# The first dense block in two halves, and the S5 parameters loaded beside the modulation

## The chip, the cores and the metric

The kernel runs on one core of one Trainium2 chip. The metric is the device time of one execution in microseconds (us). Three runs of the kernel before took 3180.70, 3186.01 and 3205.12 us; the median is 3186.01 us.

## What is computed

One step of a decoder layer is computed for a prompt of 2048 tokens and for 8 x 8 sample tokens, width 1024, all in float32. Cut to what matters here:

```python
mod = silu(c) @ w_ada + b_ada                     # c: 9 rows (prompt and 8 samples), w_ada 1024 x 6144
sh1, sc1, gt1, sh2, sc2, gt2 = split(mod, 6)      # six pieces of 1024 columns
h = rms_norm(x, norm1_g) * (1 + sc1) + sh1
q, k, v, g, u, gate_r, gate_s = split(h @ w_in)
ret = retention(rotary(q), rotary(k), v)          # gated by silu(g)
ssm = s5(u, lam, log_dt, b, c, d)                 # diagonal state space scan, complex
x = x + gt1 * (merge of ret and ssm) @ w_out
x = x + gt2 * relu(rms_norm(x) * (1 + sc2) + sh2 @ w_up)**2 @ w_down
```

No `h` exists before `sh1` and `sc1` (columns 0 to 2047 of `mod`) are known, and the S5 branch needs tables (powers of exp(lam dt), and products with b and c) that are worked out from small parameters.

## The kernel before

The prompt is worked off in four super-blocks of 512 tokens; the feed-forward part comes behind all four. A product of float32 numbers is made of three products of rounded pieces: every operand X is kept as `hi`, X rounded to the matmul's type, and `lo`, the rest.

**Weights.** `fetch` loads one unit of a weight (256 x 512, 512 KB) into a tile `wraw`, of which there are four (RAW). `refill` makes `whi` from it on ScalarE (ACT, L191) and `wlo` by a subtraction on GpSimd (POOL, L194), or on VectorE (DVE, L194) for units of `w_ada`. `block` takes the units of one 512-column product, one after the other, for four PSUM banks `pd`: with eight input tiles of 128 rows there are four units of 24 matmuls, 96 in all. `self.names` is the order of the blocks: "u", "ada4", "q", "ada5", "k", "ada6", "v", "ada7", "g", and so on. All DMAs are issued by SyncE (SP), in order, and each waits for the one eight places before it (eight semaphores, DMAHW0 to DMAHW7, taken in turn).

**The start** is `setup`. It loads the columns of `w_ada` in four pieces of 512 (`load(n)`, two tiles `wa` of 1 MB each), and the first 512 rows of x (tiles `x0`, four loads of 512 KB, L1412). Pieces 0 and 1 give `sh1`, pieces 2 and 3 give `sc1`. The loop `for q in range(2)` does the two halves of the 1024 channels: `ada(q)` and `ada(2 + q)` are the modulation products on TensorE (PE, L810, into `ps_ada`), `mod_out` adds the bias on DVE (`mt`, L843), turns the result with PE (`ptm`, L848) and copies it to `modT` (L849); `scales` works out `s1`. For each of the four tiles of x, `turn` transposes four pieces into a bank `pt` (L817) and `norm_out` scales them on DVE (`m`, L651), rounds them on ACT (`hh`, L653) and subtracts on POOL (`hl`, L654). `hh[0], hl[0]` are the first half of the channels, `hh[1], hl[1]` the second. Rows of x are first brought to unit size by sums of squares on ACT (`junk`, L605), a short chain of one-column instructions on DVE (L591 to L610) and a multiplication (L825). Then `super_block` begins with block "u", all 96 matmuls over both halves.

**The S5 set-up** is a generator, `s5_setup`: small loads first (`lam`, `s5w` for log_dt, `s5bc`, `s5cc`, L906 to L921), then two PE steps (`pl` L927, `pc` L934), then about 300 instructions on DVE. The first of these, L943, needs log_dt alone; the chain to L1020 works on 32 or 64 columns; from L1034 on tables are built and eight steps (L1104 to L1132) make the tiles that go to DRAM. `setup` runs it to its first `yield`, behind everything else. The rest is spread over the blocks by the `spawn`ed filler.

**What sets the order.** The Python code gives the order in which instructions are written, but a scheduler reorders each engine's list by its own timeline before the program is built. Each engine then runs its list strictly in order, and a waiting instruction holds up all behind it. PSUM has two pools of four banks, `pd` for the dense products and `pm` for all else.

Of the kernel before, what the change touches and what calls it, by code (L numbers as in the profile page):

```python
# [10 lines left out]
F32 = mybir.dt.float32  # L11
# [6 lines left out]
P = 128  # L18
# [64 lines left out]
class Layer:  # L83
# [150 lines left out]

    def block(self, name, kind, src, evac=None, sample=None, order="k"):
        nc = self.nc
        assert self.names[self.at] == name, (self.names[self.at], name)
        self.at += 1
        nu = 2 if name == "glu" or name[:2] in ("br", "bs") else 4
        nk = 2 * nu  # L240
        banks = [self.pd.tile([P, 512], F32, tag="pd", name=f"pd_{name}") for _ in range(4)] if kind else []
        sb = self.bank(f"ps_{name}", [P, 512]) if sample else None
# [19 lines left out]
        if order == "k":  # L262
            for u in range(nu):
                w = self.weight(name)
                for j in range(4 if kind else 0):
                    for kk in range(2):
                        products(2 * u + kk, j, w, kk)
                    if u == nu - 1:
                        evac(j, banks[j])
                    if j == 0:  # L270
                        self.refills()
                    self.tick()
                if sample:
                    for kk in range(2):
                        sample_products(2 * u + kk, w, kk)
                    if u == nu - 1:
                        self.spawn(sample[1](sb))
                    if kind is None:
                        self.refills()
                        self.tick()  # L280
                self.due += 1
                self.side()
            return
# [449 lines left out]
    def setup(self):  # L733
# [30 lines left out]
        dma(gn[8:16], i["norm2_g"].rearrange("o (k p) -> (o k) p", p=P))  # L764
        wa = [self.unit("wa") for _ in range(8)]
        wv = i["w_ada"][0].rearrange("(k p) n -> p k n", p=P)

        def load(n):
            for a in range(2):
                dma(wa[2 * n + a], wv[:, 4 * a:4 * a + 4, 512 * n:512 * n + 512])  # L770

# [7 lines left out]
        for j in range(2, 4):  # L779
            self.x_rows(xu[1][:, j - 2], 0, j)  # L780
        load(1)
        load(3)
        for _ in range(RAW):
            self.fetch()

        th = self.work("th", [9, D])
# [20 lines left out]
        def ada(n):  # L807
            pa = self.pd.tile([P, 512], F32, tag="pd", name=f"ps_ada{n}")
            for k in range(8):
# [10 lines left out]
        for q in range(2):  # L820
            ada(q)
            if q == 0:
                for j in range(4):
                    r = self.now(self.row_rstd(x[j]))
                    V.tensor_scalar(x[j], x[j], r, None, op0=ALU.mult)  # L825
                pts = [turn(q, j) for j in range(4)]
            else:
                for _ in range(2):
                    self.refill(True)
            ada(2 + q)  # L830
            self.scales(2 + q)
            for j in range(4):
                pt = turn(q, j) if q else pts[j]
                self.norm_out(pt, q, self.s1[:, :, 0], self.modT[:, 0:8, 0], self.hh, self.hl, j, nc.gpsimd)
        for _ in range(RING - 2):
            self.refill(True)
        self.late_setup = self.s5_setup()
        next(self.late_setup)

    def mod_out(self, n, p, bias):  # L840
# [3 lines left out]
        if n in (4, 5, 10, 11):  # L844
            nc.sync.dma_start(self.modd[:, 512 * n:512 * n + 512], t)
        pt = self.pd.tile([P, 4, 9], F32, tag="pd", name="ptm")
        for a in range(4):
# [617 lines left out]
    def super_block(self, b, late):  # L1465
# [39 lines left out]
        if b == 0:  # L1505
            s5 = self.spawn(self.late_setup, 2)
        self.block("u", "T", srcT(hh, hl), ev_u, S(hS, ev_us))
        if b:
# [283 lines left out]
```

## Time and profile before

| | |
|---|---|
| median of three runs | 3186.01 us |
| the profiled execution's own time | 3184.32 us |
| its span, first to last instruction | 3182.5 us |
| PE busy | 2927.9 us (92%) |
| DVE, ACT, POOL busy | 1940.6 (61%), 1219.5 (38%), 1762.7 us (55%) |
| granted TensorE clock, mean | 0.955 |

A row of a timeline has the start in us, the duration, the engine, the line of the kernel, the operation, the tile written `<-` the tiles read, the shapes and a count; in brackets how long the engine was idle before it and what ended that. A row with a count spans all its instructions. SPq rows are the issues of DMAs; their durations are those of the issue, not of the transfer. The table by windows has for each stretch the busy time of each engine with its number of instructions, the granted clock of PE, and the busy share of the DMA engines.

### The profile page before, as it was taken

How to read it: one execution, taken by the hardware profiler on the slowest of the kernel's cores; microseconds unless marked ns; L12 is line 12 of the kernel's file. 1: busy time of each engine (PE TensorE's matmuls, PEld its weight loads, DVE VectorE, ACT ScalarE, POOL GpSimd, SP SyncE). 2: the span in 40 equal slices, each digit the busy share in tenths (PEclk: the TensorE clock that was granted, in tenths of full speed). 3: DMA queues.
4: the chain of work that ended last, by engine and by line, in shares of the span. 5: the costliest groups of instructions: out<-in, count | busy, mean ns of one | idle time of the engine just before them, and what ended most of it. 6: DMA issues, size and time to landing. Idle time of an engine off the chain costs nothing. (4 is left out here: it accounts for less than half of the span.)

```text
span 3182.5 us, 37110 instructions
## 1 busy us (share of the span) xinstructions
PE 2927.9 (92%) x13436; PEld 2384.8 (75%) x13436; DVE 1940.6 (61%) x3116; ACT 1219.5 (38%) x1876; POOL 1762.7 (55%) x1028
## 2 busy tenths in 40 slices
PE   7789999999989899999999669999999999997995
PEld 3568777788777688787788558887778788875884
DVE  4978674761667865657644745545556655456654
ACT  2233442122423234432244235555334555553332
POOL 2331454434345545555356456658888666587881
PEclk9889999999999899999999889999999999998998
DMA  8466435543246854367543654446444644466442
GB/s 218 154 196 208 147 103 171 162 130 109 85 107 212 240 174 136 105 200 229 162 137 127 183 163 168 155 146 205 159 146 167 203 166 158 159 219 210 143 148 82
DMA packets 335980, 516.51 MB, mean 162 GB/s; under 512 B 71206, under 2 KB 167990, under 8 KB 331691
## 3 DMA queue, kind: packets, MB, share of 16 engines
q1 hardware_dynamic: 335796, 514.13, 51.0%
q8 instruction: 106, 1.74, 0.2%
q14 instruction: 78, 0.64, 0.1%
HBM read 399.29 MB, written 114.78 MB: 162 GB/s over the span
## 5 line engine op out<-in xcount | busy, mean ns | idle before, releaser
L194 POOL TENSOR_TENSOR wlo<-wraw,whi 128x1024 fp32r<-128x1024 f32 x248 | 614.2, 2487 | 764.3 <-ACT whi L191 646.7
L399 PE MATMUL pq_down<-shi,tw 128*128 128x512 f32 x1792 | 568.9, 397 | 36.6 <-DVE acc L459 26.4
L399 PE MATMUL pq_up<-shi,tw 128*128 128x512 f32 x1792 | 558.5, 392 | 34.9 <-ACT shi L390 26.1
L191 ACT ACTIVATE whi<-wraw 128x1024 fp32r<-128x1024 f32 x312 | 324.0, 1056 | 651.0 <-issue 72.2
L399 PEld LDWEIGHTS pq_down<-shi,tw 128*128 128x128 f32 x1792 | 342.2, 191 | 115.9 <-issue 21.9
L399 PEld LDWEIGHTS pq_up<-shi,tw 128*128 128x128 f32 x1792 | 338.6, 189 | 108.3 <-ACT shi L390 28.4
L311 POOL TENSOR_TENSOR tw<-traw,tw 128x512 fp32r<-128x512 f32 x192 | 286.5, 1507 | 210.4 <-ACT tw L310 210.1
L391 DVE TENSOR_TENSOR slo<-sw,shi 128x1024 fp32r<-128x1024 f32 x140 | 236.9, 1704 | 209.6 <-ACT shi L390 177.4
L399 PE MATMUL pq_down<-slo,tw 128*128 128x512 f32 x896 | 354.1, 395 | 0.0
L399 PE MATMUL pq_up<-slo,tw 128*128 128x512 f32 x896 | 351.0, 392 | 1.7 <-DVE slo L391 1.7
L390 ACT ACTIVATE shi<-sw 128x1024 fp32r<-128x1024 f32 x140 | 147.1, 1056 | 271.2 <-DMA sw<-sd 181.2
L459 DVE SCALAR_TENSOR_TENSOR acc<-pq_down,modT,acc 128x512 f32<-128x512 f32 x224 | 159.2, 743 | 89.7 <-PE pq_down L399 89.3
L399 PEld LDWEIGHTS pq_up<-slo,tw 128*128 128x128 f32 x896 | 169.3, 189 | 38.0 <-DVE slo L391 3.0
L399 PEld LDWEIGHTS pq_down<-slo,tw 128*128 128x128 f32 x896 | 171.4, 191 | 35.2
L310 ACT ACTIVATE tw<-traw 128x512 fp32r<-128x512 f32 x224 | 136.3, 624 | 66.5 <-PE pq_down L399 51.5
L409 ACT ACTIVATE aq<-pq_up 128x512 f32<-128x512 f32 x128 | 72.3, 591 | 194.2 <-PE pq_up L399 194.2
L345 POOL TENSOR_TENSOR ts<-traw,ts 128x512 f32<-128x512 f32 x64 | 97.6, 1525 | 57.1 <-issue 54.6
L194 DVE TENSOR_TENSOR wlo<-wraw,whi 128x1024 fp32r<-128x1024 f32 x64 | 85.8, 1340 | 69.5 <-ACT whi L191 65.5
L311 POOL TENSOR_TENSOR tw<-t,tw 128x512 fp32r<-128x512 f32 x64 | 103.3, 1624 | 32.7 <-ACT tw L310 28.7
L310 ACT ACTIVATE tw<-ts 128x512 fp32r<-128x512 f32 x128 | 80.2, 627 | 101.1 <-PE pq_up L399 80.4
L253 PE MATMUL pd_wo<-whi,mh 128*128 128x512 f32 x256 | 102.2, 403 | 12.1 <-DVE tw L1680 6.7
L437 DVE TENSOR_TENSOR sq<-aq 128x512 f32<-128x512 f32 x32 | 29.6, 925 | 130.7 <-ACT aq L414 130.7
(526 smaller groups left out, 6770.9 us busy)
## 6 DMA issues: line engine op xcount, KB each, us to landing
wraw<-in_w_in_dram SPq DMA_DIRECT2D x144, 512.0 KB
sw<-sd SPq DMA_DIRECT2D x112, 512.0 KB
s5p<-s5c SPq DMA_DIRECT2D x32, 1024.0 KB
traw<-in_w_up_dram SPq DMA_DIRECT2D x64, 512.0 KB
sd<-sq SPq DMA_DIRECT2D x32, 1024.0 KB
sd<-aq SPq DMA_DIRECT2D x32, 768.0 KB
traw<-in_w_down_dram SPq DMA_DIRECT2D x24, 1024.0 KB
wraw<-in_w_ada_dram SPq DMA_DIRECT2D x32, 512.0 KB
```

The costliest lines, as they stand in the source:

```text
L191: a = nc.scalar.activation(hi, raw, AF.Copy)
L194: l = eng.tensor_sub(lo, raw, hi)
L253: nc.tensor.matmul(banks[j], a, b, start=(k == 0 and z == 0), stop=(k == nk - 1 and z == 2))
L310: self.nc.scalar.activation(t[:, 0], x, AF.Copy)
L311: eng.tensor_sub(t[:, 1], x, t[:, 0])
L345: G.tensor_sub(x[p], l, x[m] if isinstance(m, int) else m)
L390: nc.scalar.activation(hi[:, a], t, AF.Copy)
L391: V.tensor_sub(lo[:, a], t, hi[:, a])
L399: self.nc.tensor.matmul(bank, w, x, start=(first and a == 0 and z == 0), stop=(a == 3 and z == 2), skip_group_check=True)
L409: copy = lambda d, b: nc.scalar.activation(d, b, AF.Copy)
L437: V.tensor_add(S[:, 0], A21, A22)
L459: V.scalar_tensor_tensor(d, b, g, d, op0=ALU.mult, op1=ALU.add)
```

## The change

The first block is cut in two, and what surrounds it is put in another order.

- `block` gets an argument `part`. With `part=0` it takes the first two units of the weights (channels 0 to 511, `hh[0]` and `hl[0]`) and keeps its four banks; with `part=1` it takes the other two units into the same banks and finishes.
- In `setup`, `block("u", part=0)` is written behind the first half of the normalisation, ahead of `ada(1)` and `ada(3)`; `super_block` then does `part=1`.
- The loads of pieces 1 and 3 of `w_ada` move behind the S5 parameters; two units of u's weights are fetched ahead of both.
- `s5_setup` is begun in the middle of `setup`, and run on to its third `yield` within it.
- The products `ada(1)` and `ada(3)` and their `ptm` use the pool `pm` in place of `pd`, whose four banks the first half of u keeps.

```diff
+        if part != 0:
+            self.at += 1
...
+        if part == 1:
+            banks = self.held
+        else:
+            banks = [self.pd.tile([P, 512], F32, tag="pd", name=f"pd_{name}") for _ in range(4)] if kind else []
+            self.held = banks
...
-            for u in range(nu):
+            for u in range(nu) if part is None else range(2 * part, 2 * part + 2):
...
         for j in range(2, 4):
             self.x_rows(xu[1][:, j - 2], 0, j)
-        load(1)
-        load(3)
-        for _ in range(RAW):
+        for _ in range(2):
             self.fetch()
+        self.late_setup = self.s5_setup()
+        next(self.late_setup)
...
-            pa = self.pd.tile([P, 512], F32, tag="pd", name=f"ps_ada{n}")
+            pa = self.pm.tile([P, 512], F32, tag="pm", name=f"ps_ada{n}") if n % 2 else \
+                self.pd.tile([P, 512], F32, tag="pd", name=f"ps_ada{n}")
...
             ada(q)
             if q == 0:
+                load(1)
+                load(3)
+                for _ in range(RAW - 2):
+                    self.fetch()
                 for j in range(4):
                     r = self.now(self.row_rstd(x[j]))
                     V.tensor_scalar(x[j], x[j], r, None, op0=ALU.mult)
                 pts = [turn(q, j) for j in range(4)]
             else:
-                for _ in range(2):
-                    self.refill(True)
+                next(self.late_setup)
             ada(2 + q)
...
+            if q == 0:
+                next(self.late_setup)
+                for _ in range(2):
+                    self.refill(True)
+                hh, hl = self.hh, self.hl
+                self.block("u", "T", lambda k, j: (hh[k // 4][:, k % 4], hl[k // 4][:, k % 4]), part=0)
         for _ in range(RING - 2):
             self.refill(True)
-        self.late_setup = self.s5_setup()
-        next(self.late_setup)
...
-            s5 = self.spawn(self.late_setup, 2)
-        self.block("u", "T", srcT(hh, hl), ev_u, S(hS, ev_us))
+            s5 = self.spawn(self.late_setup, 1)
+        self.block("u", "T", srcT(hh, hl), ev_u, S(hS, ev_us), part=None if b else 1)
```

What the scheduler makes of it is seen in the lists of the engines. The changed kernel has other line numbers: from `s5_setup` on they are 15 higher (L943 is now L958), L843 and L849 are now L857 and L864, L810 and L817 are now L817 and L824, and L253 is now L258.

DVE before, from the last preparation of silu(c) on: the bias of the first modulation piece (`mt`) comes next.

```order
L800 TENSOR_TENSOR cT<-z,cT 128x8x9 [waits Activation_49]
L843 TENSOR_TENSOR mt<-ps_ada_176,ba 9x512 [waits DMAHW0_49,PE_49]
L849 COPY modT<-ptm 128x36 [waits PE_49]
L609 TENSOR_SCALAR v<-ss 128x1 [waits Activation_49]
L610 TENSOR_SCALAR v<-v 128x1 [waits DVE_49]
L591 TENSOR_SCALAR y<-v 128x1 [waits DVE_49]
```

DVE after, at the same place (`s5w` holds log_dt, and DMAHW4 is the landing of its load):

```order
L806 TENSOR_TENSOR cT<-z,cT 128x8x9 [waits Activation_49]
L958 TENSOR_SCALAR s5w<-s5w 128x32 [waits DMAHW4_49]
L857 TENSOR_TENSOR mt<-ps_ada_187,ba 9x512 [waits DMAHW0_49,PE_49]
L959 TENSOR_SCALAR s5w<-s5w 128x32 [waits DVE_49]
L960 CAST s5w<-s5w 128x32 [waits DVE_49]
L961 CAST s5w<-s5w 128x32 [waits DVE_49]
L864 COPY modT<-ptm 128x36 [waits PE_49]
L614 TENSOR_SCALAR v<-ss 128x1 [waits Activation_49]
```

The first instruction of the S5 chain now stands ahead of `mt` of the first modulation product, and the rest of that chain is woven into the normalisation of x.

SP before, from the load of the third tile of x on (`x_126` are tiles 2 and 3):

```order
L1412 DMA x_126<-in_x_prompt_dram 128x1x1024 [waits DMAHW4_49]
L1412 DMA x_126<-in_x_prompt_dram 128x1x1024 [waits DMAHW5_49]
L770 DMA wa<-in_w_ada_dram 128x4x512 [waits DMAHW6_49]
L770 DMA wa<-in_w_ada_dram 128x4x512 [waits DMAHW7_49]
L770 DMA wa<-in_w_ada_dram 128x4x512 [waits DMAHW0_49]
L770 DMA wa<-in_w_ada_dram 128x4x512 [waits DMAHW1_49]
L181 DMA wraw<-in_w_in_dram 128x2x512 [waits DMAHW2_49]
```

SP after, at the same place:

```order
L1427 DMA x_118<-in_x_prompt_dram 128x1x1024 [waits DMAHW4_49]
L1427 DMA x_118<-in_x_prompt_dram 128x1x1024 [waits DMAHW5_49]
L181 DMA wraw<-in_w_in_dram 128x2x512 [waits DMAHW6_49]
L181 DMA wraw<-in_w_in_dram 128x2x512 [waits DMAHW7_49]
L921 DMA lam<-in_ssm_lambda_re_dram 32x64 [waits DMAHW0_49]
L922 DMA lam<-in_ssm_lambda_re_dram 32x64 [waits DMAHW1_49]
L921 DMA lam<-in_ssm_lambda_im_dram 32x64 [waits DMAHW2_49]
L922 DMA lam<-in_ssm_lambda_im_dram 32x64 [waits DMAHW3_49]
L924 DMA s5w<-in_ssm_log_dt_dram 128x32 [waits DMAHW4_49]
L928 DMA s5bc<-in_ssm_b_re_dram 64x32x16 [waits DMAHW5_49]
```

Nine more S5 loads follow, and then the four `wa` of pieces 1 and 3. The load of log_dt stands eight places behind that of the third tile of x, so it waits for that tile.

PE before, from the transposes of the first two tiles of x on; `ps_ada_332` is `ada(1)`:

```order
L848 MATMUL ptm<-cpk,mt 128x9 [waits DVE_49]
L848 MATMUL ptm<-cpk,mt 128x9 x3
L810 MATMUL ps_ada_332<-wa,z 9x512 [waits DMAHW6_49]
L810 MATMUL ps_ada_332<-wa,z 9x512 x3
L810 MATMUL ps_ada_332<-wa,z 9x512 [waits DMAHW7_49]
L810 MATMUL ps_ada_332<-wa,z 9x512 x3
L817 MATMUL pt<-cpk,x_126 128x128 [waits DVE_49]
```

PE after, with `ps_ada_444` for `ada(1)`, which now lies in the pool `pm`, and the first rows of block "u":

```order
L949 MATMUL pc<-cpk,s5cc 128x128 [waits DMAHW4_49,DMAHW3_49]
L949 MATMUL pc<-cpk,s5cc 128x128 x3
L817 MATMUL ps_ada_444<-wa,z 9x512 [waits DMAHW6_49,DVE_49]
L817 MATMUL ps_ada_444<-wa,z 9x512 x3
L817 MATMUL ps_ada_444<-wa,z 9x512 [waits DMAHW7_49]
L817 MATMUL ps_ada_444<-wa,z 9x512 x3
L258 MATMUL pd_u<-hh,whi 128x512 [waits Activation_49]
L258 MATMUL pd_u<-hl,whi 128x512 [waits Pool_49]
```

`ada(1)` now stands behind all four transposes of x and the S5 transposes (`pl`, `pc`) and also waits for DVE, which must empty the last of the four `pt` banks first. The 48 matmuls of u's first half follow it, then `ptm` of `ada(1)`, all of `ada(3)`, and the transposes of the second half of the channels; the other 48 matmuls of u come last.

More of the change, by code (lines that the diff above doesn't have):

```diff
@@ L233, in side, with block @@
             self.spawn(evac(st[0]))
-    def block(self, name, kind, src, evac=None, sample=None, order="k"):
+    def block(self, name, kind, src, evac=None, sample=None, order="k", part=None):
         nc = self.nc
         assert self.names[self.at] == name, (self.names[self.at], name)
-        self.at += 1
+        if part != 0:
+            self.at += 1
         nu = 2 if name == "glu" or name[:2] in ("br", "bs") else 4
         nk = 2 * nu
-        banks = [self.pd.tile([P, 512], F32, tag="pd", name=f"pd_{name}") for _ in range(4)] if kind else []
+        if part == 1:
[3 more added lines that the diff above has]
+            self.held = banks
         sb = self.bank(f"ps_{name}", [P, 512]) if sample else None
@@ L764, in setup @@
         dma(gn[8:16], i["norm2_g"].rearrange("o (k p) -> (o k) p", p=P))
-        wa = [self.unit("wa") for _ in range(8)]
+        wa = {}
         wv = i["w_ada"][0].rearrange("(k p) n -> p k n", p=P)
@@ L769, in load @@
             for a in range(2):
+                wa[2 * n + a] = self.unit("wa")
                 dma(wa[2 * n + a], wv[:, 4 * a:4 * a + 4, 512 * n:512 * n + 512])
@@ L845, in mod_out @@
             nc.sync.dma_start(self.modd[:, 512 * n:512 * n + 512], t)
-        pt = self.pd.tile([P, 4, 9], F32, tag="pd", name="ptm")
+        pool = ("pm", self.pm) if n % 2 else ("pd", self.pd)
+        pt = pool[1].tile([P, 4, 9], F32, tag=pool[0], name="ptm")
         for a in range(4):
```

## The prediction

> **What bounds the kernel now.** I read the windows first, cut at the marks of the first blocks, then the timelines of PE, DVE, ACT and SP there.
>
> ```profile
> 0.00:62.90 62.90, 41.81 (x121) 11.91 (x121) 22.27 (x76) 12.36 (x25) 9.88 (x10) 0.89 0.84 237
> 62.90:86.60 23.70, 23.70 (x109) 18.96 (x109) 22.92 (x77) 11.05 (x15) 9.84 (x6) 1.00 0.71 170
> 86.60:222.60 136.00, 105.46 (x466) 83.50 (x465) 129.19 (x258) 36.43 (x48) 47.31 (x21) 0.85 0.51 167
> 222.60:300.00 77.40, 75.09 (x416) 61.21 (x415) 62.35 (x148) 26.58 (x42) 17.67 (x7) 0.97 0.76 240
> 300.00:3182.00 2882.00, 2681.85 (x12331) 2209.18 (x12329) 1703.86 (x2561) 1133.09 (x1748) 1677.97 (x984) 0.96 0.50 158
> ```
>
> The columns are the stretch, its length, busy PE, PEld, DVE, ACT and POOL, the clock, DMA share and GB/s. From 222.6 us on PE is busy 97% of the next stretch, so it sets the pace there. Before that it lacks work: 21.1 us up to 62.9 (62.90 - 41.81) and 30.5 us between 86.6 and 222.6 (136.00 - 105.46), where DVE is busy for 129.2 of 136.0 us. The start waits for loads and normalisation, the stretch behind it for DVE, which works through the S5 set-up. The change touches only these 222.6 us, and the idle PE there, some 52 us or 1.6% of the span, is the most that it could give.
>
> ```profile
> 9.84 9.66 PE L810 MATMUL ps_ada<-wa,z 128*9 128x512 f32 x16 [1.25 <-DVE z L798]
> 20.26 0.41 PE L848 MATMUL ptm<-cpk,mt 9*128 9x9 f32 x4 [0.77 <-DVE mt L843]
> 41.06 9.40 PE L810 MATMUL ps_ada<-wa,z 128*9 128x512 f32 x16 [2.77 <-DMA wa<-in_w_ada_dram]
> 52.52 0.66 PE L817 MATMUL pt<-cpk,x 128*128 128x128 f32 x4 [0.15 <-DVE m L651]
> 54.78 7.04 PE L810 MATMUL ps_ada<-wa,z 128*9 128x512 f32 x16
> 62.92 0.50 PE L253 MATMUL pd_u<-hh,whi 128*128 128x512 f32 x1
> 86.59 0.39 PE L259 MATMUL ps_ada<-whi,cT 128*41 128x512 f32 x1
> 90.26 0.40 PE L253 MATMUL pd_q<-hh,whi 128*128 128x512 f32 x1
> 139.97 0.80 PE L253 MATMUL pd_k<-hh,whi 128*128 128x512 f32 x1 [10.23 <-DVE rt L1518]
> 210.69 0.45 PE L1116 MATMUL pw<-cpk,s5bx 128*128 128x128 f32 x1 [8.02 <-DVE s5bx L1109]
> ```
>
> Block "u" runs from 62.92 to 86.59 without a gap; its first half hides the second half of the normalisation. Between 86.59 and 90.26 stand sixteen matmuls, 0.229 us each.
>
> ```profile
> 19.53 0.68 DVE L843 TENSOR_TENSOR mt<-ps_ada,ba 9x512 f32<-9x512 f32 x1 [9.18 <-PE ps_ada L810]
> 24.80 0.75 DVE L825 TENSOR_SCALAR x<-x,y 128x1024 f32<-128x1024 f32 x1
> 61.85 0.68 DVE L843 TENSOR_TENSOR mt<-ps_ada,ba 9x512 f32<-9x512 f32 x1 [6.77 <-PE ps_ada L810]
> 63.79 5.20 DVE L651 TENSOR_SCALAR m<-pt,s,modT 128x128 f32<-128x128 f32 x16
> 68.91 0.87 DVE L943 TENSOR_SCALAR s5w<-s5w 128x32 f32<-128x32 f32 x1
> 79.40 1.22 DVE L194 TENSOR_TENSOR wlo<-wraw,whi 128x1024 fp32r<-128x1024 f32 x1
> 104.94 0.68 DVE L868 TENSOR_TENSOR mt<-mt,ps_ada 9x512 f32<-9x512 f32 x1
> 105.74 0.69 DVE L1034 TENSOR_TENSOR s5pw<-s5bc,s5w 128x512 f32<-128x512 f32 x1
> 222.58 0.16 DVE L1191 COPY s5t<-carry 128x4 f32<-128x4 f32 x1
> ```
>
> DVE begins the S5 chain at 68.91, reaches its tables at 105.74 and is through at 222.58; block "g" and with it the dense stretch follow. So two chains must be compared: when DVE gets to L1034 and from there to L1191, and whether PE has its work done by then.
>
> **The change part by part.**
>
> *The new wait.* L943 now stands ahead of the first `mt` on DVE and waits for log_dt. That load cannot be issued before the third tile of x has landed, eight places ahead of it.
>
> ```profile
> 33.82 0.63 ACT L605 ACTIVATE junk<-x 128x512 f32<-128x512 f32 x1 [9.39 <-DMA x<-in_x_prompt_dram]
> 38.67 0.63 ACT L605 ACTIVATE junk<-x 128x512 f32<-128x512 f32 x1 [3.51 <-DMA x<-in_x_prompt_dram]
> 62.70 0.42 SPq L909 DMA_DIRECT2D s5w<-in_ssm_log_dt_dram  x1
> 63.16 0.69 SPq L913 DMA_DIRECT2D s5bc<-in_ssm_b_re_dram  x1
> 72.14 0.45 SPq L1504 DMA_DIRECT2D rot<-in_rot_dram  x1
> ```
>
> The third tile is there at 33.82. In the trace of before log_dt is issued at 62.70 and used at 68.91, at most 6.2 us later. The fourth tile of x, there at 38.67, and two units of weights are in the queues ahead of log_dt. Bounds: 34 + 2, if it overtakes them, to 38.7 + 6.2 = 45. I take **39**, the fourth tile's row, since transfers mostly land in the order of issue. Behind the waiting instruction stand `mt`, all of the normalisation of x, and on PE `ptm` and `ada(2)`. So the first `mt` goes from 19.53 to 39.0, and `ada(2)` starts 1.1 us later (`mt` at 19.53 to the end of `ptm` at 20.67): 40.1.
>
> *The clock.* The four modulation products have the same work, but 9.66 and 9.40 us against 7.04: `ada(1)` came behind a pause, in a stretch with a granted clock of 0.85, `ada(3)` behind dense work.
>
> ```profile
> 40.00:60.00 20.00, 18.15 (x57) 5.66 (x58) 10.76 (x33) 4.42 (x7) 9.32 (x6) 0.85 0.69 248
> 60.00:80.00 20.00, 19.23 (x86) 14.07 (x85) 17.20 (x45) 7.98 (x10) 10.20 (x7) 1.00 0.72 153
> ```
>
> I give 9.4 us to each product behind a pause. [...]
>
> *Up to the first half of u.* `ada(2)` ends at 49.5. From `mt` to the first `m` took 1.94 us (61.85 to 63.79); with sixteen `m`, 5.20 us, two multiplications of x, 0.75 each, and a transposition of 0.66 the last `pt` is empty at 58.8, say 59. `ada(1)` needs that bank, so it starts then. Its weights are no later: the nine S5 loads from 63.16 to 72.14 keep SP for 9.0 us, here from 38.7 to 48, and 2 MB at the 237 GB/s of the first row are there by 57. `ada(1)` ends at 68.4, 48 matmuls of u at 79.4 (48 x 0.229 = 11.0).
>
> *The rest of the modulation.* `ptm` 0.4, `ada(3)` 7.04: 86.8. Then 1.94 and 5.20: DVE is done with the normalisation at **94.0**, against 69.0 before (63.79 + 5.20). The second half of u follows the last rounding, 0.65 us on ACT, at 94.7; 11.0 us and 2.4 for the clock make 108.1. Block "u" so ends **21.5 us later** than at 86.59: its first half stands alone, and no longer covers the second normalisation.
>
> *What DVE has gained.* While PE is busy from 59 to 86.8, DVE does the chain up to L1020, which before lay behind the normalisation. At 94.0 it begins L1034, before at 105.74: 11.7 us sooner. From L1034 to L1191 it needed 116.8 us. To that come four `wlo` of 1.22 (the DVE ones between 78 and 87) and two instructions for `ada4` of 0.68, which before were done by then: 6.2 us. And POOL:
>
> ```profile
> 89.58 2.44 DVE L993 TENSOR_SCALAR s5w<-s5w 128x64 f32<-128x64 f32 x1
> 99.10 0.18 DVE L993 TENSOR_SCALAR s5w<-s5w 128x64 f32<-128x64 f32 x1
> 87.75 11.35 POOL L194 TENSOR_TENSOR wlo<-wraw,whi 128x1024 fp32r<-128x1024 f32 x4 [12.01 <-ACT whi L191]
> ```
>
> The same instruction takes 2.44 us beside these four and 0.18 behind them; five instructions fill 9.5 us, a loss of about 8.8. In the changed kernel these subtractions come behind the normalisation, beside the tables; bounds 0 and 8.8. I take 3, nearer to nothing, because three of POOL's `wlo` now run beside a DVE that has time (59 to 87). 94.0 + 116.8 + 6.2 + 3 = 220.0, against 222.6: **2.6 us sooner**.
>
> *Is PE ready?* From the end of u it needs the 105.5 us of the third window: 108.1 + 105.5 = 213.6. There are 6.4 us for waits, and each pause saved gives some back through the clock. It just holds. The `part` argument, the pool of `ada(1)` and the fetches of later weights I cost at nothing: the latter hide behind u and `ada4`, and a late unit would cost its transfer, 2.2 us for 512 KB at 237 GB/s.
>
> *Sum.* The profiled execution took 3184.32 us, 1.7 below the median of the runs. 3184.3 - 2.6 = 3181.7, so **3182**. A measurement tells no change from about 1%, 32 us here.
>
> **The rivals.**
>
> *POOL gets out of DVE's way (faster).* Between 125 and 137 the same happens to two-input instructions:
>
> ```profile
> 131.46 2.82 DVE L1104 TENSOR_TENSOR s5bx<-s5bc,s5pw 128x512 f32<-128x512 f32 x1
> 136.95 0.68 DVE L1107 TENSOR_TENSOR s5bx<-s5bc,s5pw 128x512 f32<-128x512 f32 x1
> 128.18 8.30 POOL L194 TENSOR_TENSOR wlo<-wraw,whi 128x1024 fp32r<-128x1024 f32 x3
> ```
>
> Three at 2.82 or more instead of 0.68 lose 6.4 us, the shorter two ahead of them about 2. If DVE waits for PE, or reads PSUM, whenever POOL subtracts, this 8.4 and the 3 above go, and log_dt landing at 36 gives 3: 3181.7 - 14.4 = 3167. For it: the order is new. Against: POOL has as many subtractions as before, and DVE hardly a pause for them to fall into. [...]
>
> *PE becomes the bound (slower).* If the waits of 10.23 (k for the evacuation of q) and 8.02 us recur, PE reaches 222.6's place at 108.1 + 105.5 + 18.2 = 231.8, 9.2 us late: 3193.5. It decides as soon as more than 6.4 us of such waits remain. For it: u ends 21.5 us later, and q, k and v each wait for DVE to empty four banks. Against: DVE comes to q's evacuation later too, and works on the S5 steps meanwhile. A late log_dt, at 45, pushes both chains by 6 us to 3188, or 3199 together with this.
>
> *The S5 chain is not ahead.* If its instructions wait for `pl` and `pc` behind PE, they run after the normalisation as before: DVE then loses its 11.7 us, 3181.7 + 11.7 = 3193. Against: they stand ahead of `ada(1)` on PE.
>
> **How the numbers follow.** The forecast, within about 8 us, 0.5; POOL out of the way 0.2; PE the bound, with or without a late log_dt, 0.22; no lead of the S5 chain 0.05; something in the later blocks, whose order changes a little too, 0.03. The range reaches from under 3167 to the late log_dt with PE bound: 3163 to 3201. All named cases lie within 1%; for unnamed ones, the later blocks above all, I leave 0.05 faster and 0.05 slower.
>
> **What would show it.** In the changed profile the first `mt` on DVE at about 39, released by a load; `ada(2)` at 40; `ada(1)` near 59; the last `m` of the second half near 94; `ada4` near 108; L1191 at about 220; the window after it dense as before. I am wrong if log_dt lands before 34, if `ada(1)` waits for its weights past 62, if PE's waits from u to "g" exceed 6 us without a loss, or if the end differs by more than the mark at L1191 does.

## The result and the profile after

The changed kernel took 3228.95 us (median of six runs, 3216.93 to 3236.39), the kernel before, beside it, 3191.50 us (3180.70 to 3205.12). The ratio is 1.012, 95% interval 1.0099 to 1.0141: 1.2% slower, by some 37 us. The prediction, 3182 us and at most 3201, was wrong. The profiled execution took 3226.55 us, its span is 3224.7 us, 42.2 us longer than before. The traced execution of the kernel before (3184.32 us) was a quick one, 7 us under the median of its six runs, so that differences between traces come out some 5 us larger than the 37.5 between the medians. One execution of a kernel below ("early set-up, start as before") ran at a granted clock of 0.853 and took 3321.74 us; it is left out of that kernel's median.

The first instructions of VectorE that the change moved (timeline of DVE, after; line numbers of after):

```profile
40.24 0.18 DVE L958 TENSOR_SCALAR s5w<-s5w 128x32 f32<-128x32 f32 x1 [29.89 <-DMA s5w<-in_ssm_log_dt_dram]
40.34 0.67 DVE L857 TENSOR_TENSOR mt<-ps_ada,ba 9x512 f32<-9x512 f32 x1
91.70 5.20 DVE L656 TENSOR_SCALAR m<-pt,s,modT 128x128 f32<-128x128 f32 x16
96.81 1.36 DVE L1049 TENSOR_TENSOR s5pw<-s5bc,s5w 128x512 f32<-128x512 f32 x1
148.51 0.67 DVE L1531 TENSOR_TENSOR qU<-pd_q,rot 128x512 f32<-128x512 f32 x1
247.95 0.17 DVE L1206 COPY s5t<-carry 128x4 f32<-128x4 f32 x1 [2.73 <-DMA s5c<-s5pk]
```

DVE stands still for 29.89 us behind one instruction that waits for log_dt, and `mt` goes the moment it has passed. The second normalisation is done at 96.9 us (91.70 + 5.20), the tables begin at 96.81, 8.9 us sooner than before (105.74). But the end of the set-up, the last row, comes at 247.95 and not at 222.58.

PE at the start (timeline of PE, after):

```profile
41.06 0.59 PE L863 MATMUL ptm<-cpk,mt 9*128 9x9 f32 x4 [22.11 <-DVE mt L857]
41.58 8.60 PE L817 MATMUL ps_ada<-wa,z 128*9 128x512 f32 x16
59.89 1.08 PE L824 MATMUL pt<-cpk,x 128*128 128x128 f32 x4 [6.73 <-DVE x L836]
63.15 8.06 PE L817 MATMUL ps_ada<-wa,z 128*9 128x512 f32 x16
82.59 7.03 PE L817 MATMUL ps_ada<-wa,z 128*9 128x512 f32 x16
97.61 2.08 PE L258 MATMUL pd_u<-hh,whi 128*128 128x512 f32 x4 [4.84 <-ACT hh L658]
```

`ada(2)`, `ada(1)` and `ada(3)` stand 1.5 to 4.2 us behind where the prediction put them. Block u ends at 111.2 us. The windows, cut at the end of u and at the end of the first block of the gates for samples ("gs0"), first two rows before, then two after:

```profile
0.00:86.70 86.70, 65.61 (x228) 30.98 (x229) 45.28 (x153) 23.51 (x41) 19.73 (x16) 0.92 0.80 219
86.70:405.90 319.20, 284.17 (x1403) 226.87 (x1402) 255.06 (x523) 108.07 (x153) 108.31 (x48) 0.92 0.55 176
```

```profile
0.00:111.20 111.20, 67.03 (x228) 33.70 (x229) 62.60 (x248) 22.45 (x39) 20.20 (x16) 0.83 0.62 171
111.20:437.30 326.10, 286.31 (x1403) 231.47 (x1401) 249.16 (x429) 108.82 (x155) 114.17 (x48) 0.91 0.54 172
```

This is the main reading. Up to the end of u PE idled 21.1 us before (86.70 - 65.61) and 44.2 after: 23.1 more. Behind it, it idled 35.0 us before and 39.8 after: 4.8 more, where the prediction had it fall by 24 (up to the end of the set-up, from 30.5 to the 6.4 that it left for waits). With 3.6 us longer for the same matmuls, at a lower granted clock (0.83 and 0.91 where it was 0.92 in both stretches), that makes the 31.4 us by which gs0 ends later. The waits themselves (by waiter and releaser; total, times, longest), from the end of u to the end of the set-up, before and after:

```profile
PE pd_k L253 <- DVE rt L1518: 10.2, 1, 10.2
PE pw L1116 <- DVE s5bx L1109: 8.0, 1, 8.0
PE pt L874 <- DVE mt L868: 7.9, 1, 7.9
PE pd_v L253 <- DVE rt L1518: 3.7, 1, 3.7
```

```profile
PE pd_v L258 <- DVE rt L1533: 10.2, 1, 10.2
PE pt L889 <- DVE mt L883: 8.2, 1, 8.2
PE pd_k L258 <- DVE rt L1533: 7.1, 1, 7.1
PE pw L1131 <- DVE s5bx L1124: 3.2, 1, 3.2
```

The same four waits, 29.8 us before and 28.7 after, though PE came 24.5 us later to the stretch and DVE began its tables 8.9 us sooner. The 4.8 us of further idle time come behind the end of the set-up, where PE idles 4.5 us up to gs0 before and 10.1 after, most of the difference at one S5 step (before, then after):

```profile
PE py L1203 <- DVE s5t L1195: 0.2, 1, 0.2
```

```profile
PE py L1218 <- DVE s5t L1210: 5.3, 1, 5.3
```

On the side of DVE, the windows from the first table to the end of the set-up, and its waits there for ACT, before and then after:

```profile
105.74:222.58 116.84, 94.18 (x417) 75.76 (x418) 110.19 (x193) 29.08 (x39) 35.96 (x17) 0.85 0.51 167
```

```profile
DVE wlo L194 <- ACT whi L191: 0.8, 1, 0.8
```

```profile
96.81:247.95 151.14, 120.63 (x524) 95.62 (x525) 130.22 (x207) 44.56 (x59) 56.96 (x24) 0.84 0.49 157
```

```profile
DVE wlo L194 <- ACT whi L191: 11.4, 5, 4.2
```

DVE is busy 20.0 us longer in this stretch and idle 14.3 us longer (from 6.7 to 20.9). Of the idle time 10.6 us more are waits for `whi`. There are five buffers for `whi`, and ACT fills one again when PE has used it: between 150 and 248 us ACT itself stood idle for 22.3 us before four of its sixteen `whi` until PE's matmuls of k released it, and for 4.6 us before four more until those of v did. So a PE that comes late holds up DVE as well.

The remaining 10.8 us of the span arise behind the gates (gs0 to the end of the last w_out block, and the up product; before, then after):

```profile
405.90:1802.80 1396.90, 1314.45 (x6284) 1090.63 (x6283) 865.07 (x1618) 465.04 (x686) 665.78 (x316) 0.96 0.50 151
1802.80:2805.00 1002.20, 942.71 (x4131) 774.41 (x4130) 558.58 (x585) 480.56 (x754) 708.69 (x482) 0.97 0.50 169
```

```profile
437.30:1838.80 1401.50, 1319.38 (x6284) 1094.07 (x6282) 874.68 (x1618) 464.03 (x686) 665.54 (x316) 0.96 0.51 151
1838.80:2847.70 1008.90, 944.08 (x4131) 775.44 (x4130) 562.74 (x585) 480.65 (x754) 707.51 (x482) 0.97 0.49 168
```

4.6 us come in the first of these stages with PE no more idle than before, 6.7 in the second, 5.3 of them idle. In the second one wait grew: that of PE for ACT's `shi` at the start of the up product, the longest there, from 24.1 to 28.9 us. Why it grew was not settled.

### The profile page after: what moved, and what is told of

Its sections match the earlier page's. It is cut to its first block, busy times and chain, and to the rows that moved or that the text cites. A ratio compares the mean times of both kernels' runs of the same rounds, so it can differ in the third digit from the quotient of the medians.

```text
span 3224.7 us, 37113 instructions
## 1 busy us (share of the span) xinstructions
PE 2938.7 (91%) x13436; PEld 2396.9 (74%) x13436; DVE 1966.4 (61%) x3116; ACT 1218.3 (38%) x1876; POOL 1765.2 (55%) x1028
## 5 line engine op out<-in xcount | busy, mean ns | idle before, releaser
L404 PEld LDWEIGHTS pq_down<-shi,tw 128*128 128x128 f32 x1792 | 343.5, 192 | 114.6 <-issue 16.7
L404 PEld LDWEIGHTS pq_down<-slo,tw 128*128 128x128 f32 x896 | 172.0, 192 | 35.6
L258 PE MATMUL pd_wo<-whi,mh 128*128 128x512 f32 x256 | 102.7, 405 | 13.8 <-DVE tw L1695 7.6
```

The costliest lines, as they stand in the source:

```text
L258: nc.tensor.matmul(banks[j], a, b, start=(k == 0 and z == 0), stop=(k == nk - 1 and z == 2))
L404: self.nc.tensor.matmul(bank, w, x, start=(first and a == 0 and z == 0), stop=(a == 3 and z == 2), skip_group_check=True)
```

## The experiments

In the tables "u" and "gs0" are the ends of these blocks on PE against before (86.7 and 405.9 us), "idle to u" and "idle behind" PE's idle time up to u's end and from there to gs0, against before (21.1 and 35.0 us), all from the windows. The time is the median against the runs of the kernel before on the same chip. All but the time is read from one trace of each kernel. Three kernels (changed, evacuation first, and list between) have the same list on PE up to the end of u, and it comes at 111.2, 108.5 and 112.7 us: a difference of 4 us between two traces says little.

### Which part of the change costs

**log_dt first.** The changed kernel, with

```diff
+        self.s5w = self.unit("s5w", shape=(P, 32, 64))
+        dma(self.s5w[:, 0, 0:G], raw_ap(i["ssm_log_dt"], 0, [[0, P], [1, G]]))
         load(0)
...
```

> As the changed kernel, but log_dt is loaded ahead of the first piece of w_ada, so that the S5 instruction at the head of DVE does not wait and the first mt goes at about 20 us and not at 40. Theory A (what counts is when block u ends, and that lag passes on to the end in full): ada(2) starts at about 25, as before the change, the first half of the normalisation is then held by the fourth tile of x and ends at about 54 and not at 62, ada(1) starts at 55 and not at 63, and u ends near 102 and not at 111: 3229 - 9 = 3220 us. Theory B (time is lost later, by VectorE, PE and POOL waiting for one another from 97 us on, whatever the start does): the start is 9 us earlier and the end within 4 us of 3229. Theory C (the wait for log_dt is all that is wrong): 3191 us, as before.

**Block u whole.** The changed kernel without the line `self.block("u", ..., part=0)`.

> As the changed kernel, but block u is written whole behind the normalisation, so ada(3) need not come behind a half of u. Theory A: from ada(1) at 63.2 us PE has 14.1 us of ada(1) and ada(3) and 22 us of u without a pause, u ends at about 100 and not at 111, the time is 3229 - 11 = 3218 us. Theory B: within 4 us of 3229. Theory C: 3229, as log_dt is still waited for.

**The split alone.** The kernel before, with `part`, the first half of u behind the first normalisation, and the pool `pm` for the odd pieces.

> As the kernel before, but block u in two halves, the first behind ada(1), with ada(1) and ada(3) in the other PSUM pool; all loads and the S5 set-up stay where they were. ada(1) waits for the last pt bank and so starts near 50 and not at 41 us, half of u runs from 57 to 68, ada(3) to 75, the normalisation ends at 82.5, u at about 95 and not at 86.6. Theory A: 3191 + 8 = 3199 us. Theory B: VectorE begins the S5 chain at 82.5 and not at 69 and all that follows it is as much later: 3191 + 13 = 3204 us. Theory C: 3191 us, as there is no wait for log_dt.

**The early set-up alone.** Both edits of the first two together.

> As the changed kernel, but with log_dt loaded first and block u whole: of the change the early S5 set-up alone is left. Theory A: ada(1) starts at 55 us, 36 us of products follow without a pause, u ends at 91 to 92 and not at 86.6: 3191 + 5 = 3196 us. Theory B: near 3229 if the early S5 work itself upsets the stretch behind it, near 3191 if the split did. Theory C: 3191 us.

| | time | ratio, 95% | u | idle to u | idle behind | gs0 |
|---|---|---|---|---|---|---|
| changed kernel | +37.5 | 1.012 (1.0099 to 1.0141) | +24.5 | +23.1 | +4.8 | +31.4 |
| log_dt first | +31.6 | 1.0098 (1.0073 to 1.0123) | +12.6 | +9.7 | +4.5 | +18.8 |
| u whole | +26.3 | 1.0080 (1.0056 to 1.0104) | +23.1 | +20.4 | -2.6 | +21.2 |
| split alone | +35.6 | 1.0107 (1.0076 to 1.0138) | +15.6 | +14.5 | +9.5 | +28.4 |
| early set-up alone | +26.4 | 1.0082 (1.0054 to 1.0110) | +13.3 | +10.5 | -0.8 | +13.7 |

The wait for log_dt costs 12 us at the end of u (24.5 against 12.6), which theory A had put at 9, and 12.6 at gs0. Theory C, that it is all, falls, and at the gates so does B: the start does pass on. In the whole time it cannot be seen, as the intervals of the two ratios overlap (1.0073 to 1.0123, and 1.0099 to 1.0141). But the split alone and the early set-up alone are each slower than before, too. The split alone starts `ada(1)` late, as the timeline of PE shows:

```profile
52.22 1.09 PE L824 MATMUL pt<-cpk,x 128*128 128x128 f32 x4 [6.61 <-DVE x L832]
53.24 9.26 PE L817 MATMUL ps_ada<-wa,z 128*9 128x512 f32 x16
```

53.24 against 41.06 before, for in the pool `pm` it stands behind the last `pt`, and PE waited 6.61 us for that tile of x. The second normalisation then ends at 88.1, the tables begin at 126.6 (before 105.7) and gs0 comes 28.4 us late, far more than theory A's 8 and more than B's 13. The early set-up alone has its tables at 84.1 us, 21.7 sooner than before, and u 13.3 us later; gs0 is 13.7 us later. So a lead of 21.7 us on VectorE bought nothing.

The two kernels with u written whole don't take the split away, though. The scheduler still puts 48 of u's matmuls ahead of the end of the second normalisation, 23 on either side of `ada(3)`, and in the middle of u PE then waits 5.3 us for a `whi` that stands behind four `hh` in ACT's list. So u ends near 110 where 100 was expected, and at 100.1 where 92 was; that the time of "u whole" came out at +26.3, where theory A had 27, is luck. The time of the early set-up alone is 26.4 us above before, where theory A had 5: 8 us of that are lost at the end of u, the rest behind it, and its traced execution was 10 us quicker than its median. What the early set-up costs without any split is not shown here. Behind u these two idle 0.8 to 2.6 us less than the kernel before, the three with u written in halves 4.5 to 9.5 us more.

### What VectorE's lead is worth

In VectorE's list the end of the set-up has place 409 in each of these kernels, and what comes ahead of it is only dealt differently. The places, read from the lists:

| | tables | mt of ada4 | evacuation of q | of k | end |
|---|---|---|---|---|---|
| before | 216 | 212 | 277 | 335 | 409 |
| changed kernel | 203 | 278 | 316 | 344 | 409 |
| changed, evacuation first | 217 | 207 | 214 | 306 | 409 |
| changed, list between | 203 | 248 | 255 | 323 | 409 |
| chain ahead | 208 | 277 | 316 | 351 | 409 |
| chain ahead, list between | 208 | 247 | 255 | 323 | 409 |

**The evacuation first.** The changed kernel with `self.spawn(self.late_setup, 24)` in place of 1.

> As the changed kernel, but the rest of the S5 set-up is spawned 24 ticks into block u and not 1. In VectorE's list the bias of ada4 (mt) then stands at place 207 and not at 278, the evacuation of q at 214 and not at 316; the tables come behind them, the end of the set-up stays at place 409. Theory D (the waits of PE recur because VectorE's list has q's and ada4's work behind 113 and not 61 instructions of the set-up): PE's waits of 8.19 us for mt and 7.12 us for the evacuation of q go, the one for that of k grows from 10.23 to some 17 us, for it stands behind 92 instructions now: 3229 - 8 = 3221 us. Rival (VectorE has the same work to do before the S5 steps of the first super-block can start, and these steps set the time): 3229 us within 4, and PE's waits only move.

**The early set-up, PE's start as before.** The kernel before, log_dt first, the other S5 loads between `load(1)` and `load(3)`, the chain written as in the changed kernel.

> As the kernel before, with block u whole and ada(1) in the pool and at the place of before, but log_dt loaded first, the other S5 parameters loaded between pieces 1 and 3 of w_ada, and the S5 chain written between the two halves of the normalisation as in the changed kernel. PE has ada(1) near 41 us again. VectorE has 101 instructions of the S5 chain between the last m of the first half and the last m of the second, so the second normalisation may end some 8 us later than at 69. Theory A (the end follows PE's idle time at the start): u ends between 87 and 95, 3191 to 3199 us. Theory E (the lead of VectorE pays as soon as u is not late): the tables begin 10 to 20 us sooner than at 105.7, PE's four waits of 29.8 us in all between u and g shrink, and the time falls to about 3182 us.

**The chain ahead of the modulation.** The kernel before, with the following, where the first step of `s5_setup` loads lam and log_dt alone and the four steps of the loop run the chain up to the tables:

```diff
+        self.late_setup = self.s5_setup()
+        next(self.late_setup)
         load(0)
...
+        for _ in range(4):
+            next(self.late_setup)
         for q in range(2):
...
```

> As the kernel before, but lam and log_dt are loaded first of the large loads and the S5 chain up to the tables is written ahead of the modulation products, where VectorE idles for 24 of the first 40 us; the other S5 parameters stay where they were. VectorE begins the tables near 75 us and not at 105.7. Theory A: u ends 2 to 3 us later than at 86.6 (five more loads ahead of w_ada), 3194 us. Theory E: PE's waits between u and g, 29.8 us in all, shrink by about 15 us, 3191 + 3 - 15 = 3179 us. Rival D: the evacuation of q stands behind 108 instructions of the tables and not 61, so the waits stay as they were, 3194 us.

**The same with the evacuation first.** 32 in place of 2 in `spawn`.

> As the last kernel, but the rest of the S5 set-up is spawned 32 ticks into block u and not 2, so that VectorE's list has ada4's mt at place 206 and q's evacuation at 214. Theory D: the wait for mt, some 8 us, and that for q's evacuation go, and VectorE, ahead by some 20 us, has done k's by the time v needs the banks but for some 8 us: 3194 - 10 = 3184 us, or 3175 if the lead pays as well. Theory A alone: no difference from the last kernel but for what PE idles less.

**The same with a list between.** 30 in place of 2.

> As the kernel with the S5 chain ahead of the modulation products, but the rest of the set-up is spawned 30 ticks into block u (2 there, 32 in the last one): VectorE's list then has the tables from place 208, ada4's mt at 247, q's evacuation at 255, k's at 323, the end at 409 as always. Theory F (the end follows the later of two marks, the end of u on PE and the end of the set-up on VectorE, each against before; VectorE's mark is set by its work alone if its list doesn't make it wait): u ends as before, VectorE begins the tables at 74, has 138 us of work less 10 of idle time and ends near 202 and not at 222.6; of PE's waits of 25 us some 15 go. Time 3191 - 15 = 3176 us. Theory A2 (whatever VectorE gains before block g is given back at the S5 steps, which PE and VectorE do in turn): PE idles 56 us up to the gates as before, 3191 us.

**The changed kernel with a list between.** 21 in place of 1.

> As the changed kernel, but the rest of the set-up is spawned 21 ticks into block u and not 1: tables from place 203, mt of ada4 at 248 and not 278, q's evacuation at 255 and not 316. Theory F: u ends 24 us late as in the changed kernel, VectorE's tables begin at 97, its end at about 97 + 130 = 227, 5 us later than before, so only u's end counts, and PE's waits for mt and the evacuation of q (8.19 and 7.12 us) shrink to a few us: 3229 - 12 = 3217 us. Theory A2: 3229 us less the 5 that the other order gave at most, 3224 us.

| | time | ratio, 95% | u | idle to u | idle behind | gs0 |
|---|---|---|---|---|---|---|
| changed, evacuation first | +29.8 | 1.0105 (1.0082 to 1.0129) | +21.8 | +19.8 | +1.1 | +22.7 |
| early set-up, start as before | +16.7 | 1.0055 (1.0031 to 1.0080) | +5.8 | +3.9 | +0.7 | +7.6 |
| chain ahead | +5.0 | 1.0027 (1.0009 to 1.0046) | -1.0 | +0.8 | -0.4 | -1.6 |
| chain ahead, evacuation first | +11.6 | 1.0046 (1.0028 to 1.0065) | -3.6 | -0.3 | -0.1 | +0.4 |
| chain ahead, list between | -7.2 | 0.9988 (0.9962 to 1.0015) | -3.9 | -0.8 | -5.9 | -8.6 |
| changed, list between | +29.1 | 1.0087 (1.0055 to 1.0119) | +26.0 | +23.3 | -7.7 | +19.3 |

With the evacuation first in the changed kernel, PE's wait for `mt` is gone, as theory D had it, that for the evacuation of q is 4.2 us and not 7.1, and that for the evacuation of k 8.0 and not 17; but PE waits 13.9 us at the S5 steps (7.3 and 6.6), where it waited 3.2. The time lies 29.8 us above before, 7.7 less than that of the changed kernel, as D said, though the intervals of the two overlap. In the early set-up with PE's start as before, the tables begin at 87.0 us, 18.7 sooner than before, and u ends 5.8 us late, yet PE waits 8.5 us for `mt`, 8.2 for the evacuation of q and 5.2 for that of k. Theory E falls; the 16.7 us are also more than the 8 that theory A allowed, and only 7.6 of them are there at gs0.

The kernel with the chain ahead is the clearest. Its timeline of DVE and PE:

```profile
73.79 2.89 DVE L1038 TENSOR_TENSOR s5pw<-s5bc,s5w 128x512 f32<-128x512 f32 x1
124.04 0.68 DVE L1520 TENSOR_TENSOR qU<-pd_q,rot 128x512 f32<-128x512 f32 x1
```

```profile
105.97 0.59 PE L877 MATMUL pt<-cpk,mt 9*128 9x9 f32 x4 [8.79 <-DVE mt L871]
142.52 0.79 PE L253 MATMUL pd_k<-hh,whi 128*128 128x512 f32 x1 [9.70 <-DVE rt L1522]
```

VectorE begins the tables 31.9 us sooner than before, u is on time, and PE still waits 8.79 and 9.70 us and idles no less behind u (-0.4), because between the first table and the evacuation of q stand 108 instructions and 50 us, not 61 and 18. The list eats the lead: Theory E falls here, too, and rival D holds, +5.0 us where it had 3. But with the evacuation first `mt` is not waited for and the evacuation of q for 3.9 us only, and again the S5 steps take their place (10.0 and 2.9 us): 3200.82 us, where 3184 or 3175 was expected. With the list between, 47 instructions stand there, and the same waits view shows

```profile
PE pd_v L253 <- DVE rt L1522: 6.4, 1, 6.4
PE pt L877 <- DVE mt L871: 2.7, 1, 2.7
PE pd_k L253 <- DVE rt L1522: 1.3, 1, 1.3
```

instead of 3.7, 7.9 and 10.2 us before. Idle time behind u is 5.9 us less than before, where 15 were expected, and in the changed kernel the list takes 12.5 us off it (from 4.8 more to 7.7 less), where 12 were. So the order of the list alone is worth 6 to 12 us of PE's idle time up to gs0 in these traces. In the whole time that is not shown: the intervals of the kernels with and without it overlap (0.9962 to 1.0015 and 1.0009 to 1.0046; 1.0055 to 1.0119 and 1.0099 to 1.0141). The best of these kernels, chain ahead with the list between, is 8.6 us ahead at gs0 and gives 7.3 of it back by the end of the first w_out block, where PE waits 4.4 us longer for VectorE to empty its banks (waits there, this kernel, then before):

```profile
PE pd_wo L253 <- DVE tw L1684: 7.5, 1, 7.5
```

```profile
PE pd_wo L253 <- DVE tw L1680: 3.1, 2, 2.0
```

Its time cannot be told from that of the kernel before.

### The split with `ada(1)` in its place, and less work on VectorE

**`ada(1)` ahead of the half.** The split alone, but `ada(1)` written ahead of the first half of u, in the pool `pd`.

> As the kernel before with block u in two halves, but ada(1) is written ahead of the first half and keeps the pool and place of before; only ada(3) is in the other pool, and its place on PE is two matmuls into u. ada(1) near 41 us, ada(3) near 55, u ends at 87 to 89. If the split as such costs, by the order of what follows u, then as much as in the kernel with the split alone less the 12 us of ada(1): 3221 - 12 = 3209 us. If its whole price was the place of ada(1) and through it the late normalisation: 3191 us.

3216.90 us against 3191.40: ratio 1.0074 (1.0051 to 1.0097). u ends 7.8 us late and not 1 to 2, and PE idles 7.6 us more behind it, gs0 +20.1. The place of `ada(1)` was 8 of the 15.6 us at u's end, not all; PE still waits 4.90 us between the halves of u, and the tables begin at 114.5. Neither price expected is met, the time being 25.5 us above before where 18 and 0 were said; the split as such costs.

**The subtractions for w_ada on GpSimd.**

```diff
-            eng = nc.vector if name == "ad" or name in SIDE and self.split % 4 < 2 else nc.gpsimd
+            eng = nc.vector if name in SIDE and self.split % 4 < 2 else nc.gpsimd
```

> As the first of these four, and the subtractions for units of w_ada, of which 16 of 1.22 us stand in VectorE's list before the end of the set-up, are done by GpSimd. If VectorE's work bounds this stretch, 16 x 1.22 = 19 us less of it would bring the end of the set-up 10 to 19 us forward, and the time to 3176 - 10 = 3166 us. If GpSimd's subtractions stretch VectorE's instructions beside them as they did before the change (2.82 us in place of 0.68), as much is lost: 3176 us or more.

3228.94 us: ratio 1.0109 (1.0060 to 1.0158), 45 us slower than its parent. Windows, the parent in two pieces up to gs0, then this kernel in one:

```profile
0.00:82.90 82.90, 62.60 (x221) 30.29 (x222) 55.84 (x236) 20.42 (x35) 20.20 (x16) 0.96 0.83 222
82.90:397.30 314.40, 285.32 (x1409) 228.28 (x1408) 238.03 (x441) 111.97 (x159) 106.91 (x48) 0.93 0.57 180
```

```profile
0.00:425.70 425.70, 355.13 (x1629) 264.69 (x1630) 304.84 (x643) 132.98 (x193) 207.64 (x96) 0.91 0.59 176
```

VectorE has 643 instructions in place of 675 (236 + 441, less two that both windows count), 32 fewer of 1.22 us (16 of them up to the end of the set-up, as the expectation counted), and is busy 304.8 us in place of 293.9. So GpSimd's 32 subtractions stretched VectorE's other work by some 50 us (10.9 + 32 x 1.22), 1.6 us each. The rows bear it out: taking as usual the median time of an instruction's form while GpSimd is idle, 61 of VectorE's instructions up to gs0 took at least 0.5 us longer than usual, in the parent 33, and every one of them overlaps a GpSimd instruction.

### Delaying one engine alone

Left open by all these: in each of them both engines' starts and the lists changed together. In the two that follow one engine is given more work; the scheduler deals the lists anew even so.

**PE 10.5 us later.**

```diff
+        pz = self.bank("dum", [P, 512])
+        for k in range(12):
+            self.tc.keep_in_program_order(nc.tensor.matmul(pz[:9], z[:, k % 8, 0:9], wa[6 + k % 8 // 4][:, k % 4], ...))
```

> As the kernel before, with twelve more products of the kind of a modulation product on PE in the middle of block u, which nobody reads: 12 x 0.88 = 10.5 us (7.04 us for eight), so that u ends that much later; nothing else is written differently. Theory S, that of the prediction (behind u PE has 30 us of waits for VectorE, and a later u only shortens them): 3191 us. Theory P (the waits recur, since the scheduler puts ada4's mt, at place 243 of VectorE's list and not 212, and the evacuation of q, at 299 and not 277, further behind the tables): 3191 + 10.5 = 3202 us.

**VectorE 10.5 us later.**

```diff
+        for _ in range(14):
+            self.tc.keep_in_program_order(V.tensor_scalar(dum, dum, l2[:, 0:1], None, op0=ALU.mult))
...
```

> As the kernel before, with fourteen more multiplications of a 128x1024 tile on VectorE beside the first part of the S5 chain, which nobody needs: 14 x 0.75 = 10.5 us; nothing else is written differently. If VectorE's work sets the end of the set-up and that sets the time: 3191 + 10.5 = 3202 us. If PE's way alone counts, and VectorE has slack: 3191 us.

With PE later: 3196.81 against 3188.61, ratio 1.0024 (1.0008 to 1.0039), u +9.4, gs0 +7.6. With VectorE later: 3200.21, ratio 1.0042 (1.0022 to 1.0062), u -4.3, end of the set-up +12.3, gs0 +14.0. The waits of PE behind u in the kernel with PE later:

```profile
PE pd_k L253 <- DVE rt L1521: 9.5, 1, 9.5
PE pt L877 <- DVE mt L871: 4.2, 1, 4.2
PE pw L1119 <- DVE s5bx L1112: 4.0, 2, 3.7
PE pd_v L253 <- DVE rt L1521: 2.6, 1, 2.6
```

20.3 us in place of 29.8 there, and the set-up ends at 225.17 us, only 2.6 later than before. But PE then idles longer at the S5 steps (5.4 us for `s5t`, 0.2 before, and 3.0 with no releaser shown), and of 9.4 us only 1.8 are won back by gs0. The time is 8.2 us longer, between 2.6 and 12.4 by the interval, so theory S falls and theory P holds for the most part. The list changed with it: as the scheduler reckons with a later PE, it puts `mt` of ada4 at place 243 and not 212, the evacuation of q at 299 and not 277, and the tables begin at 95.8 us, 10 sooner. In the other kernel the 10.5 us of work came with a list that has `mt` of ada4 far ahead of the tables, and these begin 16.9 us late, at 122.65; 12.3 of that are there at the end of the set-up and 14.0 at gs0, and PE waits 20.1 us for the evacuation of q, where it waited 10.2. Neither engine waits out the other's delay. What a delay costs with both lists as they were was not run.

## Why the prediction was wrong, step by step

**The new wait, `ada(2)`:** right. `mt` at 40.34 where 39 was said, `ada(2)` at 41.58 (40.1). log_dt, issued at 32.85, landed behind the fourth tile of x and the two units of weights issued ahead of it: the issues that wait for these three on SP went out at 36.19, 37.24 and 39.29 us.

**The clock:** 8.60 and 8.06 us for the products behind a pause, at a granted clock of 0.81 and 0.87, where 9.4 was taken, and 7.03 for `ada(3)`, at 1.00; the mean granted clock up to u's end fell from 0.92 to 0.83. No run shows the 2.4 us for the clock in u's second half as the price of a pause; they are the difference of two rows of before (9.40 - 7.04), and the half took 13.6 us at a granted clock of 0.81, 2.6 more than the 11.0. The step is of the right kind; it is small in the sum.

**`ada(1)`, the normalisation, u:** right in order, 3 to 4 us short. `ada(1)` at 63.15 (59), since the multiplication of the last tile of x came late, and `pl` and `pc` went ahead of it; the last `m` at 96.9 (94.0); u ends at 111.2 (108.1). The 11.0 us and 2.4 for its second half were right (97.61 to 111.2, 13.6).

**What DVE has gained:** the tables began at 96.81 (94.0), 8.9 us sooner than before. From there the sum took the 116.8 us of before and 9.2 more; it was 151.1 (247.95 - 96.81), 25.1 us more than the sum's 126.0. That was the first half of the failure, and the terms can be measured. The further instructions, 6.2 in the sum, took some 7 us (20.0 more of busy time less 13.0 of contention). POOL's contention, 3 in the sum, took 13.0. VectorE's idle time, 6.7 us within the 116.8, was left as it was and grew to 20.9, since VectorE waits for weights that a late PE holds up: 14.3 us that the sum had at nothing. The prediction saw that q's evacuation comes later on DVE too, and left the list unread between 94 and 220.

**"It just holds":** the step that failed. PE was given 105.5 us of work behind u and 6.4 us for waits, because the four waits of 29.8 us were taken for slack that a later PE uses up. They came back as 28.7 us. From the end of u to the end of the set-up it took 136.0 us before and 136.8 after (111.2 to 247.95). Had the step taken that stretch as fixed, the sum would have been 3184.3 + 21.5 = 3206 by its own end of u. Of the 20.7 us from there to the traced 3226.55, 3.0 are the later end of u, 6.9 the longer way from it to gs0, and 10.8 lie behind the gates. The kernel before with PE delayed agrees at gs0, where 7.6 of 9.4 us are passed on, though not at the end of the set-up, where 2.6 are.

**POOL's contention, 3 us:** too small. What VectorE's instructions beside a GpSimd one took above their usual time (the median of the form while GpSimd is idle) grew from 18.8 to 31.8 us between the first table and the end of the set-up: 13.0, beyond the bound of 8.8. VectorE's whole busy time up to gs0 rose from 300.3 to 311.8 us with the same 675 instructions. All 45 of them that took at least 0.5 us more than usual overlap a GpSimd instruction, such as these (DVE and POOL, after):

```profile
113.13 2.43 DVE L1091 TENSOR_TENSOR s5pw<-s5sa 128x32 f32<-128x32 f32 x1
112.98 9.63 POOL L194 TENSOR_TENSOR wlo<-wraw,whi 128x1024 fp32r<-128x1024 f32 x4 [11.28 <-ACT whi L191]
```

and the kernel with 32 more subtractions on GpSimd has 61 such. The instruction over 32 columns took 2.43 us, about as long as one of the four subtractions beside it (9.63 us in all), and the four others of its kind on this line, with GpSimd idle, took 0.21 to 0.22. VectorE's instructions that read a PSUM bank kept their usual time beside GpSimd: of 71 (38 before, 33 after, up to gs0) none took more than 0.02 us longer, while of the others beside GpSimd 37 of 77 and 45 of 94 took at least 0.5 longer. The rival, POOL getting out of the way, did not come true.

**The rivals:** "PE becomes the bound" was the case, and was under-priced: it took two of the four waits and netted them against a slack that was not there, 9.2 us where 25 came. "The S5 chain is not ahead" did not happen. The range ended at 3201, because its upper end was worked out from that rival.

**Behind the gates** 10.8 us more were lost that no step foresaw. All kernels of this study lose there, 4 to 26 us in their profiled runs, including those that were early at the gates; a part may be that the traced execution of the kernel before was 2 to 7 us quicker than the medians of its runs. The lists of later blocks change with every edit of the start; which of these changes costs, and whether it is the lists, was not settled.

## What to carry to other kernels

Waits of two engines for each other, seen in a trace, are no slack to count on when both work through static lists in turn: here a lag of 24.5 us grew to 31.4 at gs0, and one of 9.4 came out as 7.6. Take the length of such a stretch, up to the first block behind it in which neither waits for the other, as fixed until the new lists say otherwise; all these runs had lists dealt anew, so it is a rule of thumb and not a law. Before counting a lead, read how many instructions stand in the new list between the work that is early and the next instruction that the other engine waits for. An instruction moved to an idle engine is free only if its input is there: here one wait for 128 bytes per row held up VectorE for 29.9 us.

## What the runs showed of the hardware beyond that

Moving 32 subtractions of 1.22 us each from VectorE (busy 293.9 us up to gs0) to the idler GpSimd (127.1 us) made VectorE busier, not less busy (304.8 us): by an estimate from these numbers, some 1.6 us of stretching for each. And PE's busy time up to gs0 hardly depended on when it worked: 349.8 us before, at a mean granted clock of 0.92, 353.3 after, at 0.89, and 347.8 and 347.9 at 0.93 and 0.94 in two kernels with the chain ahead; the most in any kernel with the same matmuls was 355.2, at 0.90. That is a span of 2.1%.
